# Adaptive max pooling on one core: both large stores moved to ScalarE's DMA queue, in another order and another cut

## The chip, the cores and the metric

The kernel runs on one core of one Trainium2 chip. The core has engines with queues of their own; three of them matter here. VectorE (DVE in the profile) does all the arithmetic. SyncE (SP) and ScalarE (ACT) only issue transfers; the profile calls their DMA queues q1 and q10. Both queues are served by the same 16 DMA engines. TensorE does nothing, and GpSimd only writes a few constants at the start.

The metric is the device time of one execution in microseconds. The kernel before takes 334.97 us (median of 3 runs, 334.92 to 335.0).

## The reference

```python
batch, channels, length = 32, 256, 4096      # float32
output_size = 256

for i in range(output_size):
    start = int(i * length / output_size)
    end = int((i + 1) * length / output_size)
    result[:, :, i] = np.max(x[:, :, start:end], axis=-1)
```

4096 / 256 = 16, so every window has exactly W = 16 elements and no two overlap. The input is 134.22 MB, the output 8.39 MB. One output number is the maximum of 16 neighbouring float32 numbers, 64 bytes.

## The kernel before

**Tiling.** All 2,097,152 windows are numbered in order of memory and dealt out over the 128 partitions, `total` = 16384 windows to a partition. They come in two groups, each contiguous in memory. In group A a partition holds 13436 windows: loads of 128 (`FIRST`), twelve of 1024 (`CHUNK`) and one of 1020. In group B it holds 2948: two loads of 1024 and one of 900 (`last`). A load brings the same number of windows to every partition, one row to each; a row of 1024 windows is 65,536 bytes, the 900 windows are 57,600 bytes. Within group A the loads run from the end of each row to its front, within group B from front to end.

**Buffers.** `ring` holds two slots of 1176 windows (1024 + `GAP` = 152). Loads other than the first alternate between the two slots, and within a slot between its lower and its upper end (`moved`), so that a load overlaps only a part of what the load two before it left there. `kept` holds the maxima of everything but the last load, 15484 numbers per partition. The maxima of the last load go into the top of its own slot in `ring` (`last_kept`), beside what is being read.

**Reductions.** `pooled` (line 54) is one VectorE instruction, `reduce_max` over the 16 elements of each of n windows. A full load is reduced by two of them, of 872 and 152 windows, the one first whose region the next load into that slot needs. The last load is reduced by one of 900.

**Order of issue.** SyncE issues the first load (line 87), then the 16 others (line 96), each when the reduction that frees its region is done and the earlier load of that region has landed. Behind the last load on the same queue it issues the two stores of `kept` (line 117): first group A's (13436 numbers or 53,744 bytes a row, 6.88 MB), whose maxima have long been there, and then group B's first 2048 numbers (8,192 bytes a row, 1.05 MB), when the load before the last has been reduced. ScalarE issues one transfer in the whole kernel (line 114): the store of the last 900 numbers (3,600 bytes a row, 0.46 MB), when the last reduction is done. `tc.no_sync_barrier()` between them is a line for the scheduler of the program, not an instruction; the semaphores that order engines and transfers are put in by the framework from the regions that each operation reads and writes.

**Names for the end of the kernel.** Counted without `FIRST`, loads have numbers 0 to 15 (`n_loads`); number 14 is "the load before the last", number 15, with the 900 windows, "the last load". The long store is group A's.

Of the kernel before, what the change touches and what calls it, by code (L numbers as in the profile page):

```python
# [1 line left out]

# [4 lines left out]


@with_exitstack
def kernel(  # L10
    ctx: ExitStack,
    tc: tile.TileContext,
    x: bass.AP,
    output_size: bass.AP,
    out: bass.AP,
):

    nc = tc.nc
    P = nc.NUM_PARTITIONS
    fp32 = mybir.dt.float32

    B, C, L = x.shape
    O = int(output_size)  # L30
    assert L % O == 0, (L, O)
    W = L // O
    total = B * C * O // P
    assert B * C * O % P == 0

    CHUNK = 1024
    GAP = 152
    FIRST = 128
    LOADS_A, LOADS_B = 13, 2

    LESS = 4
    group_a = [FIRST] + [CHUNK] * (LOADS_A - 1) + [CHUNK - LESS]
    last = total - sum(group_a) - LOADS_B * CHUNK
    group_b = [CHUNK] * LOADS_B + [last]
    assert 0 < last and last * (W + 1) <= CHUNK * W

    pool = ctx.enter_context(tc.tile_pool(name="pool", bufs=1))
    ring = pool.tile([P, 2 * (CHUNK + GAP) * W], fp32, tag="ring", name="ring")
    kept = pool.tile([P, total - last], fp32, tag="kept", name="kept")

    xw = x.flatten_outer_dims().rearrange("r (o w) -> (r o) w", w=W)
    ow = out.flatten_outer_dims().rearrange("r o -> (r o)")

    def pooled(dst, at, n):

        nc.vector.reduce_max(  # L56
            out=dst,
            in_=ring[:, at * W : (at + n) * W].rearrange("p (n w) -> p n w", w=W),
            axis=mybir.AxisListType.X,
        )  # L60

    taken = 0

    def group(n):

        nonlocal taken
        span = slice(taken * P, (taken + n) * P)
        taken += n
        return (
            xw[span].rearrange("(p n) w -> p (n w)", p=P),  # L70
            ow[span].rearrange("(p n) -> p n", p=P),
        )

    stores = []
    n_loads = 0
    base = 0
    for g, loads in enumerate((group_a, group_b)):
        xg, og = group(sum(loads))
        a = sum(loads) if g == 0 else 0
        for n in loads:  # L80
            if g == 0:
                a -= n
            xn = xg[:, a * W : (a + n) * W]
            dst = kept[:, base + a : base + a + n] if n != last else None
            if n == FIRST:

                nc.sync.dma_start(  # L87
                    out=ring[:, CHUNK * W : (CHUNK + n) * W], in_=xn
                )
                pooled(dst, CHUNK, n)  # L90
            else:

                low = n_loads % 2 * (CHUNK + GAP)
                moved = n_loads // 2 % 2
                at = low + moved * GAP
                nc.sync.dma_start(out=ring[:, at * W : (at + n) * W], in_=xn)
                if n != last:
                    cut = CHUNK - GAP if moved else GAP
                    parts = [(0, cut), (cut, n)]
                    for u, v in parts if moved else parts[::-1]:  # L100
                        pooled(dst[:, u:v], at + u, v - u)
                else:
                    end = (at + CHUNK) * W
                    last_kept = ring[:, end - n : end]
                    pooled(last_kept, at, n)
                n_loads += 1
            if g:
                a += n
        full = a - last if g else sum(loads)
        stores.append((og[:, 0:full], kept[:, base : base + full]))  # L110
        base += full
    assert taken == total

    nc.scalar.dma_start(out=og[:, full : full + last], in_=last_kept)
    tc.no_sync_barrier()
    for dst, src in stores:
        nc.sync.dma_start(out=dst, in_=src)


# [1 line left out]
_INS = ['x', 'output_size']  # L121
_OUTS = [((32, 256, 256), 'float32')]

_NUMBERS = {'output_size': 256}


# [26 lines left out]
```

## Time and profile before

| | us |
|---|---|
| median of the times | 334.97 |
| span of the profiled execution, first to last instruction | 333.1 |
| what the median has beyond that span | 1.9 |
| VectorE busy (83% of the span) | 276.5 |
| VectorE idle, waiting for loads | 51.5 |
| the last load: issued, landed | 290.99, 21.6 later |
| the long store: issued, landed | 291.37, 37.2 later |
| the 1.05 MB store: issued, landed | 312.94, 18.1 later |
| the 0.46 MB store: issued, landed | 328.00, 4.2 later |

Times within the profile count from its first instruction. The profile has its own single execution; its time is the span with what lies around it, so sums are made against 333.1 and the 1.9 us are added. Busy time is an instruction's own time; the DMA's share is the mean over 16 engines. A transfer's time to landing runs from its issue on the queue to the last of its completion records, waiting in the queue included. A row of a transfer is one packet on one DMA engine, and each transfer leaves one 4-byte record per engine as well: 128 + 16 = 144 packets.

### The profile page before, as it was taken

To read this page: it belongs to the slowest core of one execution; us is meant where nothing else is said; L and a number is where in the kernel's file an instruction comes from. 1 tells how busy PE (TensorE), PEld (TensorE's weight loads), DVE (VectorE), ACT (ScalarE), POOL (GpSimd) and SP (SyncE) were. 2 spreads that over 40 slices of the span, in tenths; PEclk is the share of its full clock that TensorE was granted. 3 is DMA by queue.
4 is the path that set the end of the run, shared out by engine and by line. 5 is a ranking of instruction groups with operands and counts; after the bars stand their busy time and mean duration, and the time that the engine had idled before them with its cause. 6 is when DMAs were issued, how large, how long until landed. Compare 5 with 4: busy or idle time off the path is not lost.

```text
span 333.1 us, 113 instructions
## 1 busy us (share of the span) xinstructions
DVE 276.5 (83%) x32; POOL 0.2 (0%) x4
## 2 busy tenths in 40 slices
DVE  2009979797997979799797979979797998979993
POOL 0000000000000000000000000000000000000000
DMA  9898989899898989899898989899898989899996
GB/s 378 378 504 378 504 378 496 386 441 441 378 504 378 504 378 496 386 457 425 378 504 378 504 378 504 378 441 441 385 494 377 504 378 504 378 458 443 421 413 285
DMA packets 2880, 142.61 MB, mean 428 GB/s; under 512 B 320, under 2 KB 320, under 8 KB 448
## 3 DMA queue, kind: packets, MB, share of 16 engines
q1 hardware_dynamic: 2736, 142.15, 98.8%
q10 hardware_dynamic: 144, 0.46, 0.3%
HBM read 134.22 MB, written 8.39 MB: 428 GB/s over the span
## 4 chain that ended last, share of the span: by engine, by line
DMA 57%; DVE 36%; DVEq 5%; issue 0%; SPq 0%
DMA ring<-in_x_dram 57%; DVE kept L56 36%; DVEq L148 5%; SPq L87 0%
## 5 line engine op out<-in xcount | busy, mean ns | idle before, releaser
L56 DVE TENSOR_REDUCE kept<-ring 128x152 f32<-128x2432 f32 (+3 forms) x31 | 261.4, 8472 | 51.5 <-DMA ring<-in_x_dram 51.5
L56 DVE TENSOR_REDUCE ring<-ring 128x900 f32<-128x14400 f32 x1 | 15.1, 15144 | 0.0
L134 POOL MEMSET const-bfloat16-1.0<- 128x1 bf16 x1 | 0.1, 102 | 0.0
L134 POOL MEMSET const-uint8-127<- 128x1 uint8 x1 | 0.1, 102 | 0.0
L134 POOL MEMSET const-float32-0.0<- 128x1 f32 x1 | 0.1, 99 | 0.2 <-issue 0.2
L134 POOL MEMSET const-float32-1.0<- 128x1 f32 x1 | 0.1, 99 | 0.0
## 6 DMA issues: line engine op xcount, KB each, us to landing
ring<-in_x_dram SPq DMA_DIRECT2D x1, 8160.0 KB, 23.9
ring<-in_x_dram SPq DMA_DIRECT2D x1, 7200.0 KB, 21.6
out_dram<-kept SPq DMA_DIRECT2D x1, 6718.0 KB, 37.2
ring<-in_x_dram SPq DMA_DIRECT2D x1, 1024.0 KB, 4.7
out_dram<-kept SPq DMA_DIRECT2D x1, 1024.0 KB, 18.1
out_dram<-ring ACTq DMA_DIRECT2D x1, 450.0 KB, 4.2
ring<-in_x_dram SPq DMA_DIRECT2D x14, 24.0
```

The costliest lines, as they stand in the source:

```text
L56: nc.vector.reduce_max(out=dst, in_=ring[:, at * W : (at + n) * W].rearrange("p (n w) -> p n w", w=W), axis=mybir.AxisListType.X,)
L134: nc = _bacc.Bacc("TRN2", target_bir_lowering=False, num_devices=1)
L148: with _tile.TileContext(nc) as tc:
```

## The change

Three things change at the end of the kernel.

1. The load before the last is cut at 828 (`OPEN`) and 196 (`late`) windows instead of 872 and 152. The maxima of the 828 go into `kept` as before; those of the 196 go into the top of the last load's slot in `ring`, just ahead of the 900 maxima of the last load. So `last_kept` is now 1096 numbers long. The order of the windows on VectorE is the same.
2. Group B's first store is now 1024 + 828 = 1852 numbers a row (7,408 bytes, 0.948 MB) and needs only the reduction of the 828. The last store is 1096 numbers a row (4,384 bytes, 0.561 MB). The long store keeps its rows.
3. Queues and order: ScalarE issues group B's first store and then, behind it, the long store. SyncE, behind the last load, issues only the last store.

```diff
+    OPEN = 828
+    late = CHUNK - OPEN
     kept = pool.tile([P, total - last], fp32, tag="kept", name="kept")
+    assert last * (W + 1) + late <= CHUNK * W
...
                 nc.sync.dma_start(out=ring[:, at * W : (at + n) * W], in_=xn)
-                if n != last:
+                if n_loads == LOADS_A + LOADS_B - 1:
+                    pooled(dst[:, 0:OPEN], at, OPEN)
+                    opened = at + OPEN
+                elif n != last:
                     cut = CHUNK - GAP if moved else GAP
                     parts = [(0, cut), (cut, n)]
                     for u, v in parts if moved else parts[::-1]:
                         pooled(dst[:, u:v], at + u, v - u)
                 else:
                     end = (at + CHUNK) * W
-                    last_kept = ring[:, end - n : end]
-                    pooled(last_kept, at, n)
+                    last_kept = ring[:, end - n - late : end]
+                    pooled(last_kept[:, 0:late], opened, late)
+                    pooled(last_kept[:, late:], at, n)
                 n_loads += 1
             if g:
                 a += n
-        full = a - last if g else sum(loads)
+        full = a - last - late if g else sum(loads)
         stores.append((og[:, 0:full], kept[:, base : base + full]))
...
-    nc.scalar.dma_start(out=og[:, full : full + last], in_=last_kept)
+    nc.scalar.dma_start(out=stores[1][0], in_=stores[1][1])
     tc.no_sync_barrier()
-    for dst, src in stores:
-        nc.sync.dma_start(out=dst, in_=src)
+    nc.scalar.dma_start(out=stores[0][0], in_=stores[0][1])
+    nc.sync.dma_start(out=og[:, full : full + late + last], in_=last_kept)
```

## The prediction

> **What bounds the kernel now.** I read the page first, then the DMA queues in short windows of the tail, then the vector engine's instructions by shape, and last the first microseconds, for how long an issued transfer takes to reach the DMA engines.
>
> ```profile
> DVE 276.5 (83%) x32; POOL 0.2 (0%) x4
> ...
> DMA  9898989899898989899898989899898989899996
> q1 hardware_dynamic: 2736, 142.15, 98.8%
> q10 hardware_dynamic: 144, 0.46, 0.3%
> ...
> out_dram<-kept SPq DMA_DIRECT2D x1, 6718.0 KB, 37.2
> ...
> out_dram<-kept SPq DMA_DIRECT2D x1, 1024.0 KB, 18.1
> out_dram<-ring ACTq DMA_DIRECT2D x1, 450.0 KB, 4.2
> ```
>
> These are lines of the page. The 16 DMA engines are busy 98.8% + 0.3% = 99.1% of a 333.1 us span; the missing 0.9% is 3.0 us. VectorE is busy 83% and is the bound nowhere but, perhaps, at the very end. q1 is SyncE's queue, q10 ScalarE's: 2736 is 19 transfers of 144 packets, so each engine gets 8 rows and one 4-byte record of completion per transfer.
>
> The page's chain of waits names DMA and VectorE alternately and hides that the DMA never rests; the windows show it. Columns: stretch and length, VectorE and GpSimd busy, TensorE's clock, DMA share, GB/s. A packet is counted where it starts, so only stretches with small rows, or whole rounds of long ones, read as shares.
>
> ```profile
> 0.00:1.72 1.72, 0.00 (x0) 0.20 (x4) 1.00 0.00 0
> 1.72:2.30 0.58, 0.00 (x0) 0.00 (x0) 1.00 1.14 240
> ...
> 309.50:310.05 0.55, 0.55 (x1) 0.00 (x0) 1.00 4.17 1676
> 310.10:311.84 1.74, 1.74 (x2) 0.00 (x0) 1.00 0.00 0
> 311.84:312.30 0.46, 0.46 (x1) 0.00 (x0) 1.00 4.34 1869
> 327.70:328.15 0.45, 0.27 (x1) 0.00 (x0) 1.00 0.88 364
> 328.15:330.20 2.05, 0.00 (x0) 0.00 (x0) 1.00 1.00 420
> 330.20:330.56 0.36, 0.00 (x0) 0.00 (x0) 1.00 0.85 338
> 330.57:331.72 1.15, 0.00 (x0) 0.00 (x0) 1.00 0.79 313
> 331.72:333.10 1.38, 0.00 (x0) 0.00 (x0) 1.00 0.00 0
> ```
>
> The 3.0 us are 1.7 before the first packet and 1.4 after the last one (331.72). Between them there is nothing to win by order alone. In the tail: the 16 engines take up the last row of the last load at 309.50 to 310.05, and none starts anything until 311.84; from 311.84 to 312.30 each goes straight on to the long store (6.88 MB), which has been queued since its issue at 291.37. By queue, 311.84 to 327.7 holds 144 packets at 434 GB/s: 15.85 us for the long store. At 327.70 to 328.15 the engines go on to the 1.05 MB store, at 330.20 to 330.56 to the last one, on q10. So 2.45 us and, to 331.72, 1.15 us. The last lands at its issue, 328.00, plus 4.2 = 332.2; 0.9 us of closing follow.
>
> ```profile
> L56 DVE TENSOR_REDUCE kept<-ring 128x872 f32<-128x13952 f32 x14 | 205.6, 14686 | 44.0 <-DMA ring<-in_x_dram 44.0
> L56 DVE TENSOR_REDUCE kept<-ring 128x152 f32<-128x2432 f32 x15 | 40.1, 2676 | 0.0
> L56 DVE TENSOR_REDUCE ring<-ring 128x900 f32<-128x14400 f32 x1 | 15.1, 15144 | 0.0
> ```
>
> ```profile
> 295.63 17.28 DVE L56 TENSOR_REDUCE kept<-ring 128x872 f32<-128x13952 f32 x2 [2.07 <-DMA ring<-in_x_dram]
> 312.82 15.14 DVE L56 TENSOR_REDUCE ring<-ring 128x900 f32<-128x14400 f32 x1
> ```
>
> VectorE, by shape and in order of time: 872 + 152 windows of the load before the last, then the 900 of the last, with no idle time ahead of them; done at 327.96.
>
> **The change part by part.** The profiled span of 333.1 lies 1.87 us under the median of 334.97; I add the same 1.87 to the forecast span.
>
> *The reductions.* A window costs (14686 - 2676)/720 = 16.68 ns, so 828 windows take 14686 - 44 x 16.68 = 13952 ns and 196 take 3410 ns. Three instructions and 1924 windows as before: the 900 still start at 312.82 if the last load has landed by then (it does so at 290.99 + 21.6 = 312.6) and end at 327.96. The 196 now write into the ring; a wait of VectorE on itself for that may cost between 0 and some 0.1 us (the 900 have such a write already and start without idle time). I take 0.
>
> *The first store on ScalarE.* The 828 end at 295.63 + 13.95 = 309.58; ScalarE issues 0.04 later, as it does now behind the 900 (327.96 to 328.00): 309.62, for 0.37 us. How long until its rows are at the engines? Nearest row: the first load, issued at 0.73, shows its first packets from 1.72 to 2.30, 1.0 to 1.6 us later. Farthest: the last store, issued at 328.00, shows its first at 330.20, 2.2 us. The first gives 310.6 to 311.2, the second 311.8. In either case the engines have the last row in hand, since they took it up by 310.05 and let go of it from 311.84 on. I take the first row, as there nothing stands in the way; hole in the DMA: 0, and by the second reading at most some 0.3 us on the last engines.
>
> *The long store, now second on ScalarE.* It loses its place behind the last load on q1, held since 291.37, and is issued at about 310.0 to 310.4, at the engines by 312.2 at the latest. The first store's 0.948 MB (1852 windows) cover them for 2.45 x 1852/2048 = 2.22 us, until 314.06 to 314.52. So it costs nothing; without that cover it would be up to 0.4 us. Then 15.85 us: 329.91 to 330.37. ScalarE has nothing else to do, so its wait holds up nothing but these two; SyncE no longer stands behind the 152 windows to issue a store.
>
> *The last store, now on SyncE.* 1096 windows, 0.561 MB: 1.15 x 1096/900 = 1.40 us, against 1.15 + 2.45 - 2.22 = 1.38 that byte and packet counts leave (same bytes, same number of rows as before). Issued at 328.00, at the engines 329.0 to 329.6, or 330.2 by the far row; needed at 329.91 to 330.37. Cost 0, at the far end some 0.2 us. Its packets end at about 331.3 to 331.75, it lands at 332.2, the span ends at 333.1.
>
> The far row has two readings: from 328.15 to 330.20 all 105 packets were q1's, so either the store came late or it was there and q1's transfer was finished first. The Trainium skill ("DMA: Bandwidth & Descriptors", Queues, rings and completion order) says that a DMA engine takes turns between queues only after a whole packet of some 9 to 17 descriptors, and a share here has 9. By that rule the store had been there and waited, and the sum is +0; by the other reading it is +0.2 to +0.3 us. No run here tells the two apart.
>
> Sum: 0, between -0.15 (below) and +0.5 us: **335.0 us**, its own range 334.7 to 335.5.
>
> **The rivals.**
>
> *Slower: the last load's records wait behind the new store.* Now two queues hold work when the engines finish the last load. The 4-byte record that reports the load is q1's, and the first store's rows are there before it is sent. If an engine serves q10's 8 rows first, the load lands 2.22 us later, at 314.8; the 900 end at 329.99, the last store is issued at 330.03, at the engines 331.0 to 331.6, which have been dry since 329.91 to 330.37. End of packets 331.6 + 1.4 = 333.0, span 334.4, **336.2 us**; 337 with 2.2 us to the engines. It decides only once the load lands later than about 313.6 (330.37 - 1.57 - 0.04 - 15.14); a turn of one row (2.22/8 = 0.28 us) does nothing. Against it: those 105 packets of q1, 0 of q10, at a time when q10's store should have been there. For it: that store may not have been there.
>
> *Slower: the hand-over runs dry,* that is, the rows are not ready while the last row is in hand. The queue ahead of the engines was 20 us deep and is now 0.6 to 1.2 us (311.84 less 310.6 to 311.2). From an issue-to-engine time of 2.7 us on, all engines idle, and each further microsecond is one at the end, as the last store's own delay hides behind it. At 3.5 us: 0.8 us, **335.8 us**. Against it: 2.2 us is the most that the trace shows, and that may be a wait in turn.
>
> *Faster.* The rows of the last load took 2.13 us each in the round before (60.9% of 3.5 us) but 2.29 in the last round (4.17 x 0.55): the change from reading to writing costs 0.16 us now, with 53.7 KB rows queued behind. Short rows behind it may spare that: -0.15, **334.8 us**, which is still no change that can be told. For more than 0.2% (0.67 us) the 19.9 us of the tail would have to run 3.4% faster, while share and rate show neither a hole nor a row that is slow for its size.
>
> **How the numbers follow.** 0.2%, 0.67 us, is about what a measurement of this kernel tells from no change. Forecast, with the small gain counted in (within 0.2%): 0.78. Records behind the store, 336.2: 0.09. Hand-over dry, 335.8: 0.07. A tail faster by over 0.2%, below 334.3, by something that I do not see: 0.06. So 0.06 faster, 0.78 same, 0.16 slower. The range runs from the gain's end with a little more, 334.5, to the first slower case, 336.2.
>
> **What would show it.** Right: no stretch without DMA work between 309 and 331.7; q10's first packets of 7.4 KB follow the last load's rows at 311.8 to 312.3; the last load lands at about 312.6 and the 900 start at 312.8 to 313.0; the long store's rows start by 314.5; q1's last 4.4 KB rows follow from 329.9 to 330.4; span 333.1. Wrong: the last load landing later than 313.6, idle time of VectorE ahead of the 900, a DMA share below 1 at 312 or at 330, or long rows that take other than 15.85 us in all.

## The result, and the profile after

The changed kernel takes 335.65 us (median of 11 runs, 335.54 to 335.86) where the kernel before takes 334.98 (11 runs): a ratio of 1.0021, with a 95% interval of 1.0013 to 1.0029. It is slower by 0.67 us, which is just the 0.2% that was taken for the limit of what can be told. The 335.0 forecast were 0.65 too low; the time lies within the range.

From the page of the changed kernel:

```profile
span 333.8 us, 112 instructions
...
DMA  9898989898998989898989989898989899899996
...
q1 hardware_dynamic: 2592, 134.78, 93.5%
q10 hardware_dynamic: 288, 7.83, 5.5%
...
out_dram<-kept ACTq DMA_DIRECT2D x1, 6718.0 KB, 21.6
...
out_dram<-kept ACTq DMA_DIRECT2D x1, 926.0 KB, 6.1
out_dram<-ring SPq DMA_DIRECT2D x1, 548.0 KB, 5.0
```

The shares of the queues add up to 99.0% of 333.8 us, 330.5 us; before, 99.1% of 333.1 was 330.1. So the DMA engines as a body are hardly busier. The order of time at the end (start, length, engine, line, what):

```profile
295.48 13.95 DVE L64 TENSOR_REDUCE kept<-ring 128x828 f32<-128x13248 f32 x1 [2.06 <-DMA ring<-in_x_dram]
309.35 18.47 DVE L64 TENSOR_REDUCE ring<-ring 128x196 f32<-128x3136 f32 x2
309.46 0.37 ACTq L126 DMA_DIRECT2D out_dram<-kept  x1
309.87 3.11 ACTq L128 DMA_DIRECT2D out_dram<-kept  x1
327.85 0.35 SPq L129 DMA_DIRECT2D out_dram<-ring  x1
```

VectorE's side came out as forecast: 13.95 us for the 828 windows, no idle time ahead of the 196 or the 900, and the last store issued at 327.85, 37.0 us after the last load (290.85), as before (328.00 and 290.99). The last store then lands 5.0 us after its issue where it took 4.2, at 332.85 instead of 332.2: all of the loss is between that issue and that landing. What stands out is the 3.11 us that ScalarE spends on issuing the long store.

The same execution in windows (stretch and length, VectorE, GpSimd, clock, DMA share, GB/s):

```profile
309.50:310.05 0.55, 0.55 (x1) 0.00 (x0) 1.00 3.88 1676
311.60:312.05 0.45, 0.45 (x1) 0.00 (x0) 1.00 1.09 264
312.05:314.00 1.95, 1.95 (x2) 0.00 (x0) 1.00 0.93 391
314.00:314.40 0.40, 0.40 (x1) 0.00 (x0) 1.00 4.98 2145
314.40:315.05 0.65, 0.65 (x1) 0.00 (x0) 1.00 0.05 23
315.05:315.15 0.10, 0.10 (x1) 0.00 (x0) 1.00 1.25 537
...
331.85:332.35 0.50, 0.00 (x0) 0.00 (x0) 1.00 0.04 18
```

And by queue, from 311.60 to 312.05 and from 312.05 to 313.90 (packets, MB, share of 16 engines):

```profile
q10 hardware_dynamic: 16, 0.12, 107.0%
q1 hardware_dynamic: 16, 0.00, 2.0%
```

```profile
q10 hardware_dynamic: 98, 0.73, 93.0%
```

In 311.60 to 312.05 every engine finishes the last load, sends its record (q1's 16 small packets) and takes up the first row of ScalarE's store. These 16 rows take 107.0% x 0.45 = 0.48 us each; the rows behind them 93.0% x 1.85 x 16 / 98 = 0.28. So a first row takes 0.20 us longer, on the mean; a packet's time runs from when its engine takes it up, so the engine counts as busy while it waits. That is why no hole shows. One of the 16 can be singled out, from 311.965 to 311.970 (a packet's whole time is put where it starts, hence the share over 100%):

```profile
q10 hardware_dynamic: 1, 0.01, 1488.8%
```

That is 1488.8% x 0.005 x 16 = 1.19 us for one row, 0.9 too long; with seven more rows its engine would be done with the first store at 315.1. One engine is indeed that far behind the rest: by 314.40 fifteen have gone on to the long store, and the sixteenth does so only after 315.05 (the window 314.40 to 315.05 holds its last two short rows and nothing else). Its eight rows at 0.28 us take 2.25, so its data began to move at about 312.85, 3.4 us after the issue at 309.46. With 15.85 us for the long store and eight rows of the last store at 0.17 us it would be done at 315.10 + 15.85 + 1.4 = 332.3, and at the far end one engine is again alone, in 331.85 to 332.35. So this one engine sets the end.

### The profile page after: what moved, and what is told of

It reads as the page before. It is cut to its first block, busy times and chain, and to the rows that moved or that the text cites. A ratio compares the mean times of both kernels' runs of the same rounds, so it can differ in the third digit from the quotient of the medians.

```text
span 333.8 us, 112 instructions
## 1 busy us (share of the span) xinstructions
DVE 276.5 (83%) x32; POOL 0.2 (0%) x4
## 4 chain that ended last, share of the span: by engine, by line
DMA 57%; DVE 36%; DVEq 5%; issue 0%; SPq 0%
DMA ring<-in_x_dram 57%; DVE kept L64 35%; DVEq L160 5%; DVE ring L64 1%; SPq L95 0%
## 5 line engine op out<-in xcount | busy, mean ns | idle before, releaser
L64 DVE TENSOR_REDUCE kept<-ring 128x152 f32<-128x2432 f32 (+4 forms) x30 | 258.1, 8641 | 51.4 <-DMA ring<-in_x_dram 51.4
L64 DVE TENSOR_REDUCE ring<-ring 128x196 f32<-128x3136 f32 (+1 forms) x2 | 18.5, 9276 | 0.0
## 6 DMA issues: line engine op xcount, KB each, us to landing
ring<-in_x_dram SPq DMA_DIRECT2D x1, 8160.0 KB, 23.9
ring<-in_x_dram SPq DMA_DIRECT2D x1, 7200.0 KB, 21.6
out_dram<-kept ACTq DMA_DIRECT2D x1, 6718.0 KB, 21.6
```

The source lines that it names most:

```text
L64: nc.vector.reduce_max(out=dst, in_=ring[:, at * W : (at + n) * W].rearrange("p (n w) -> p n w", w=W), axis=mybir.AxisListType.X,)
```

## The experiments

All times are compared with runs of the kernel before on the same chip (medians of 334.95 to 335.08 us). The numbers in brackets are the 95% interval of the ratio; 0.0009 of it is 0.3 us, so differences of 0.1 or 0.2 us between two runs mean nothing by themselves. Each edit is against the changed kernel.

### SyncE issues all three stores

```diff
-    nc.scalar.dma_start(out=stores[1][0], in_=stores[1][1])
+    nc.sync.dma_start(out=stores[1][0], in_=stores[1][1])
...
-    nc.scalar.dma_start(out=stores[0][0], in_=stores[0][1])
+    nc.sync.dma_start(out=stores[0][0], in_=stores[0][1])
```

> Cut and order of the changed kernel, but SyncE issues all three stores: first store, long store, last store. Changed kernel 335.65 us, before 334.98. Theory 'jam' (the long store's issue, which took 3.11 us on ScalarE, blocks the descriptors of the store ahead of it for one DMA engine, whatever the queue): SyncE's second issue also takes about 3 us and one engine's first row is 0.9 us late, 335.6. Theory 'queue change' (an engine that goes over from q1 to another queue pays, one of them 0.9 us): everything stays on q1, nobody pays, 335.0. Theory 'too late' (the rows come only 2.2 us ahead of their use): same as changed, 335.6.

335.06 us, 0.11 over before (ratio 0.9995 to 1.0012). From its order of time:

```profile
309.63 0.35 SPq L126 DMA_DIRECT2D out_dram<-kept  x1
310.03 0.43 SPq L128 DMA_DIRECT2D out_dram<-kept  x1
```

Cut, order and lead are the changed kernel's, and the loss is gone: it lies with the queue. The long store is issued in 0.43 us. The first rows of 7.4 KB take 0.29 us: 311.70 to 311.98 holds 11 of them and 11 records at a share of 72.4%, 3.24 us of packets. Both "too late" and "jam" expected a loss here whatever the queue, and are wrong in that form.

### The long store back on SyncE

```diff
-    nc.scalar.dma_start(out=stores[0][0], in_=stores[0][1])
+    nc.sync.dma_start(out=stores[0][0], in_=stores[0][1])
```

> Cut of the changed kernel; ScalarE issues the first store alone, SyncE the long store (right behind the last load, at about 291) and then the last store. 'Jam': ScalarE has no second issue, so no row is late: 335.0. 'Queue change': the engines go over to q10 and back somewhere, one of them pays 0.7 to 0.9 us: 335.6. 'Too late': the long store fills the time until the rows are there, 335.0.

335.05 us, 0.10 over before (0.9995 to 1.0013): nobody pays, though ScalarE's queue is used. The windows 311.7 to 313.7 and 313.70 to 316.00 by queue bear on something that the prediction rested on:

```profile
q1 hardware_dynamic: 32, 0.86, 99.9%
```

```profile
q1 hardware_dynamic: 16, 0.86, 86.3%
q10 hardware_dynamic: 16, 0.12, 12.2%
```

In the first window each engine takes up one long row behind the load's record, and none of ScalarE's, issued at 309.53. In the second they take 16 long rows and 16 short ones, and on to 329.7 it is 112 and 116. With work on two queues the engines here take turns row by row. They do not finish one queue's share of a transfer first, and a store issued some 2.2 us ahead is not yet in the turn.

### Earlier: OPEN = 700

```diff
-    OPEN = 828
+    OPEN = 700
```

> The changed kernel with OPEN = 700 instead of 828: the first store (5.6 KB rows) is issued 128 x 16.68 ns = 2.1 us earlier, at about 307.3, with one more row of the last load to come. 'Too late': no row is late any more, 335.0. 'Jam': the long store's issue on ScalarE takes about 5 us instead of 3.1, and one engine still starts late, 335.6. 'Queue change': same as changed, 335.6. If the engines change queues in the middle of a transfer's rows, the first store's rows start ahead of the last load's last row and the load lands up to 1.7 us late; nothing comes of it as long as the last reduction starts before 313.6.

335.22 us, 0.27 over before (0.9999 to 1.0017). Issued at 307.60, the first rows take their normal time, 64.0% x 0.26 x 16 / 10 = 0.27 us for rows of 6.9 KB. ScalarE's second issue took 4.47 us, nearly the 5 that "jam" expected, yet the first rows are not late. That speaks for "too late" and against the jam. The last load lands 21.9 us after its issue instead of 21.6: its record has to let one short row of q10 pass, as turns by row demand.

### The cut alone

```diff
-    nc.scalar.dma_start(out=stores[1][0], in_=stores[1][1])
+    nc.scalar.dma_start(out=og[:, full : full + late + last], in_=last_kept)
     tc.no_sync_barrier()
-    nc.scalar.dma_start(out=stores[0][0], in_=stores[0][1])
-    nc.sync.dma_start(out=og[:, full : full + late + last], in_=last_kept)
+    for dst, src in stores:
+        nc.sync.dma_start(out=dst, in_=src)
```

> The cut alone (828 and 196 windows, 7.4 KB and 4.4 KB rows); queues and order as before: SyncE the long store and then the first store, ScalarE the last one. All theories: 335.0, as before. If it gives 335.6, the cut is the cause and not the queues.

334.94 us against 334.95 (0.9992 to 1.0009). The cut and its shorter rows are worth nothing, either way.

### ScalarE's queue used once before

```diff
-                nc.sync.dma_start(
+                nc.scalar.dma_start(
                     out=ring[:, CHUNK * W : (CHUNK + n) * W], in_=xn
                 )
```

> The changed kernel (335.65 us, one engine's first 7.4 KB row 0.9 us late), but the very first load of the kernel comes from ScalarE, so that its queue q10 has been used once, long before. Theory 'first use' (an engine is late because q10 is used for the first time): no late row, 335.0. Theories 'jam' (the long store's issue is stuck 3.1 us behind the first store on ScalarE) and 'too late' (q10's rows need over 2.2 us to be in place on the slowest engine): no change, 335.6. The first load's 8 KB rows may alternate with those of the second load and land at 20 us or so instead of 5; the first reduction comes later by that, which the 2 us of idle time per load take up.

338.34 us (1.0082 to 1.0113), worse by another cause. The first load landed 24.8 us after its issue instead of 4.6, as its rows took turns with the long ones of the second load; the first reduction began at 25.6, and the DMA share fell to 0.65 from 40 to 44 us. I had thought that the idle time of VectorE takes this up, and it does not. So its time says nothing on the question. Its trace does. By queue, 313.50 to 314.50, which holds 14 of the 16 first rows of the first store in this run:

```profile
q10 hardware_dynamic: 14, 0.10, 68.6%
```

68.6% x 1.0 x 16 / 14 = 0.78 us for a first row, though q10 had been used at the kernel's start: it is not the first use. The other way round it falls too: with OPEN = 764 or 700, and with short rows in hand, q10 is used for the first time and is not late. In this run the late rows do not lengthen the tail: the first store lands 24.0 us after the last load's issue (312.44 + 5.4 - 293.82), as in the kernels without a loss, and not 24.7 as in the changed kernel. By this, late rows cost time only where they make the slowest engine later.

### The last store on ScalarE too

```diff
-    nc.sync.dma_start(out=og[:, full : full + late + last], in_=last_kept)
+    nc.scalar.dma_start(out=og[:, full : full + late + last], in_=last_kept)
```

> The changed kernel with the last store on ScalarE too, behind the long one: no change of queue at the end. The changed kernel's last store had first rows of 0.26 to 0.32 us where 0.17 is the rule, and SyncE's kernel (all on q1) none. 'Change of queue costs 0.1 us at the end, the late engine 0.7': 335.5. If the late engine has its cause at the end and not at the first store: 335.0.

335.84 us, 0.76 over before (1.0013 to 1.0030). Without the change of queue at the end the loss is still there; the first rows of the first store (311.8 to 312.45) take 109.8% x 0.65 = 0.71 us, on the mean. The cause lies at the first store.

### The first store alone on ScalarE

```diff
-    nc.scalar.dma_start(out=stores[0][0], in_=stores[0][1])
-    nc.sync.dma_start(out=og[:, full : full + late + last], in_=last_kept)
+    nc.sync.dma_start(out=og[:, full : full + late], in_=last_kept[:, 0:late])
+    tc.no_sync_barrier()
+    nc.sync.dma_start(out=stores[0][0], in_=stores[0][1])
+    nc.sync.dma_start(
+        out=og[:, full + late : full + late + last], in_=last_kept[:, late:]
+    )
```

> ScalarE issues the first store alone; nothing stands behind it on either queue until SyncE, when the 196 windows are reduced (312.8), issues three stores: those 196 (784 B rows), the long one, the last 900. 'Jam': without a second issue on ScalarE no first row of 7.4 KB is late (none over 0.5 us). 'Too late': the same engine is late again, with a first row of about 1.2 us. The time is not the test: the long store is issued at 313.2 and the first store ends at 314.1, so 0.1 to 1.3 us without DMA work are added in any case, 335.1 to 336.3, and 0.9 more on one engine only if the late row is there and not hidden by that.

335.92 us, 0.84 over before (1.0016 to 1.0033). By queue, 311.80 to 312.38:

```profile
q10 hardware_dynamic: 16, 0.12, 117.8%
```

117.8% x 0.58 = 0.68 us for a first row, with no second issue behind it. So the jam on ScalarE is not the cause; that it is another effect of the same thing is likely and not shown.

### Earlier by half as much: OPEN = 764

```diff
-    OPEN = 828
+    OPEN = 764
```

> The changed kernel with OPEN = 764: the first store is issued 64 x 16.68 ns = 1.07 us earlier than with 828, 3.2 to 3.6 us ahead of its first use instead of 2.2 to 2.5. With 828 the time was 335.65, with 700 335.22. 'Too late': with 3.2 us no first row is late, 335.0 to 335.2. 'Jam': the late row of 0.9 us is there as with 828, 335.6.

335.36 us, 0.28 over before (0.9999 to 1.0017). The issue at 308.74, some 3.2 us ahead of its first use, is early enough, and an issue earlier by another microsecond (OPEN = 700) gains nothing more. Whether the 0.28 that are left are a cost at all is open: the interval reaches down to no change.

### OPEN = 764, and the last store on ScalarE

```diff
-    OPEN = 828
+    OPEN = 764
...
-    nc.sync.dma_start(out=og[:, full : full + late + last], in_=last_kept)
+    nc.scalar.dma_start(out=og[:, full : full + late + last], in_=last_kept)
```

> OPEN = 764 (first store 1.07 us earlier, 335.36 alone, 0.28 over its kernel before) and the last store on ScalarE too, behind the long store. Theory 'a queue that stood idle behind long rows starts late' (lead of 2.2 to 2.5 us is too short for such a queue, 3.2 us is enough; a queue that is at work needs no more than 2.1): neither the first store's first rows nor the last store's are long, and the time is 0.0 to 0.15 us over before, 335.0 to 335.2. If the 0.28 come from the earlier issue itself (the last load's record waits behind a row of the first store, landing 0.5 us later), they stay: 335.3.

335.01 us, 0.04 over before (0.9993 to 1.0010): with both taken away no cost is left that can be told. By queue, 311.70 to 311.98 of this kernel:

```profile
q10 hardware_dynamic: 13, 0.09, 80.1%
```

80.1% x 0.28 x 16 / 13 = 0.28 us, a row's normal time. The last store's first rows differ too. On SyncE's idle queue with OPEN = 764 (329.99 to 330.27, 10 rows of q1 at 70.5%) they took 0.32 us; here, on the queue that has just sent the long store (329.82 to 330.05, 12 rows and 11 records at 61.4%), 0.18. That the last load's record comes later costs nothing: it landed 22.0 us after its issue here too. But neither do the longer first rows of the last store show as the cause of the 0.28: in the profiled execution with OPEN = 764 the last store lands 41.2 us after the last load's issue (328.32 + 4.1 - 291.19), here 41.3 (328.21 + 4.1 - 291.05), in the kernel before 41.2 (328.00 + 4.2 - 290.99). What is longer there lies ahead of the last load, which is issued at 291.19 instead of 290.99, and there the two kernels are the same.

### Short rows in hand

```diff
-                nc.sync.dma_start(out=ring[:, at * W : (at + n) * W], in_=xn)
+                for u, v in ((0, 700), (700, n)) if n == last else ((0, n),):
+                    nc.sync.dma_start(
+                        out=ring[:, (at + u) * W : (at + v) * W],
+                        in_=xn[:, u * W : v * W],
+                    )
```

> The changed kernel (OPEN = 828, +0.67 us), but the last load is issued in two pieces of 700 and 200 windows, so that the engines have rows of 12.8 KB (0.48 us each) in hand and not of 57.6 KB (2.13 us) when the first store is issued. 'Idle queue behind long rows': with short rows in hand the first store's rows are in place in time, no first row over 0.35 us, +0.2 (the last store's 0.1 stays). 'Idle queue alone', whatever stands in front: first rows of up to 1.2 us again, +0.7.

335.32 us, 0.35 over before (0.9999 to 1.0017). From its order of time, and by queue from 311.80 to 312.08:

```profile
309.60 0.37 ACTq L130 DMA_DIRECT2D out_dram<-kept  x1
310.01 0.44 ACTq L132 DMA_DIRECT2D out_dram<-kept  x1
```

```profile
q10 hardware_dynamic: 12, 0.09, 75.9%
```

Issued as late as in the changed kernel, the first rows take 75.9% x 0.28 x 16 / 12 = 0.28 us, and the second issue is not stuck. So in these runs the idle queue is late only when the engines have long rows in hand. That fits the kernel before, whose last store on the idle q10 follows rows of 8 KB: its first 27 rows of 3.6 KB took 66.5% x 0.36 x 16 / 27 = 0.14 us each in 330.20 to 330.56, no longer than the later ones.

### Later: OPEN = 872

```diff
-    OPEN = 828
+    OPEN = 872
```

> The changed kernel with OPEN = 872, the cut of the kernel before: the first store is issued 44 x 16.68 ns = 0.73 us later. 'Too late': the time until its rows move stays what it is, so every engine stands idle for about 0.73 us more, and the time goes from +0.67 to +1.2 to +1.4 us, 336.2 to 336.4. 'A fixed price of the change of queue': no change, +0.7.

335.76 us, 0.79 over before (1.0015 to 1.0034). From 311.70 to 312.50:

```profile
q10 hardware_dynamic: 16, 0.12, 144.1%
```

Now a first row takes 144.1% x 0.8 = 1.15 us on the mean, 0.87 too long on every engine. That every engine pays more is what "too late" expected; that the time is only 0.12 longer than with 828, no difference that can be told, is not. The slowest engine is no later than before: measured from the last load's issue, the first store lands 24.7 us later (310.54 + 5.3 - 291.17), as with 828 (309.46 + 6.1 - 290.85). So the lead that an engine needs is not one fixed time: some 2.3 us here on the mean (issue 310.54, taken up at about 312.0, 0.87 waited), 3.4 for the slowest with 828. What sets it on one engine is open.

### SyncE and ScalarE swapped in every transfer

```diff
-                nc.sync.dma_start(
+                nc.scalar.dma_start(
                     out=ring[:, CHUNK * W : (CHUNK + n) * W], in_=xn
                 )
...
-                nc.sync.dma_start(out=ring[:, at * W : (at + n) * W], in_=xn)
+                nc.scalar.dma_start(out=ring[:, at * W : (at + n) * W], in_=xn)
...
-    nc.scalar.dma_start(out=stores[1][0], in_=stores[1][1])
+    nc.sync.dma_start(out=stores[1][0], in_=stores[1][1])
     tc.no_sync_barrier()
-    nc.scalar.dma_start(out=stores[0][0], in_=stores[0][1])
-    nc.sync.dma_start(out=og[:, full : full + late + last], in_=last_kept)
+    nc.sync.dma_start(out=stores[0][0], in_=stores[0][1])
+    nc.scalar.dma_start(out=og[:, full : full + late + last], in_=last_kept)
```

> The changed kernel with SyncE and ScalarE swapped in every transfer: ScalarE issues all loads and the last store, SyncE the first store and the long one. If it is the idle queue that starts late, SyncE's first rows are now as long as ScalarE's were (up to 1.2 us), +0.7. If it is ScalarE or its queue, no first row is over 0.35 us: +0.1 to +0.3.

335.71 us, 0.74 over before (1.0014 to 1.0032). In 311.80 to 312.33 SyncE's first rows now take 130.3% x 0.53 = 0.69 us, and it is SyncE that is stuck in the second issue:

```profile
309.80 0.37 SPq L126 DMA_DIRECT2D out_dram<-kept  x1
310.22 2.99 SPq L128 DMA_DIRECT2D out_dram<-kept  x1
```

```profile
q1 hardware_dynamic: 16, 0.12, 130.3%
```

It is the idle queue and not the engine that issues.

The kernels side by side. Issue and landing are counted from the issue of the last load, each landing being the sum of issue and time to landing, from the one profiled execution; the last column is the time over the kernel before. The engines finish the last load's rows some 21.0 us after its issue (311.60 to 312.05 less 290.85 in the changed kernel), so a first store issued at 18.6 has a lead of some 2.4 us. In the kernel before the last store lands at 41.2.

| kernel | queue of the first store | rows in hand | first store issued | first store lands | last store lands | over before |
|---|---|---|---|---|---|---|
| all on SyncE | at work | 57.6 KB | 18.6 | 23.9 | 41.2 | +0.11 |
| OPEN = 700 | idle | 57.6 KB | 16.5 | 23.8 | 41.3 | +0.27 |
| OPEN = 764, all on ScalarE | idle | 57.6 KB | 17.6 | 24.0 | 41.3 | +0.04 |
| OPEN = 764 | idle | 57.6 KB | 17.6 | 23.9 | 41.2 | +0.28 |
| short rows in hand | idle | 12.8 KB | 18.6 | 24.0 | 41.3 | +0.35 |
| changed kernel | idle | 57.6 KB | 18.6 | 24.7 | 42.0 | +0.67 |
| all on ScalarE | idle | 57.6 KB | 18.6 | 24.4 | 41.7 | +0.76 |
| first store alone on ScalarE | idle | 57.6 KB | 18.6 | 24.4 | 41.8 | +0.84 |
| swapped | idle | 57.6 KB | 18.6 | 24.6 | 41.9 | +0.74 |
| OPEN = 872 | idle | 57.6 KB | 19.4 | 24.7 | 41.8 | +0.79 |

In the upper five the first store lands at 23.8 to 24.0 us and the last one at 41.2 to 41.3, as in the kernel before; in the lower five the first lands at 24.4 to 24.7 and the last at 41.7 to 42.0. Within a group the times differ by about as much as they are uncertain, and part of that lies ahead of the last load: it is issued at 290.85 in the changed kernel and at 291.31 with all stores on ScalarE, which differ only behind it. None of the runs beats the kernel before: its engines are never idle, and order alone wins nothing, as the sum had it.

## Why the prediction was right, and where not

**The bound, and "no change" as the likeliest: right in substance.** The order of the stores is free, as the DMA's work is the same: the version with both delays taken away is at +0.04 us, the cut alone at -0.01. The sum of 0 holds for the parts that it has. That the measured 335.65 still lies within the full range is in part luck: its upper end, 336.2, was taken from another rival, the records behind the store, which did not happen; the sum's own range ended at 335.5.

**The reductions: right.** 13.95 us, the 900 without idle time ahead of them, the last store issued 37.0 us after the last load.

**The first store on ScalarE: this step failed.** I took 1.0 to 1.6 us from issue to engine, from the first load of the kernel, "as there nothing stands in the way", and thereby chose the wrong of two rows: in the tail a 57.6 KB row stands in the way on every engine. The far row, 2.2 us, was nearer to the truth and still too short: 2.3 to 2.6 us on the mean and 3.4 on the slowest engine. I bounded the hole by "some 0.3 us on the last engines"; it was 0.20 on the mean, but 0.9 on one, and the slowest of 16 sets the end. That is why the forecast's own range ended short of the 335.65.

**The long store behind it: harmless, but not as said.** I had it at the engines by 312.2 at the latest; its issue alone took 3.11 us, to 312.98. The first store's rows cover that, as the sum had it: fifteen engines went on to the long store at 314.0 to 314.4.

**The weighed rule: wrongly applied.** By the Trainium skill ("DMA: Bandwidth & Descriptors", Queues, rings and completion order) a whole packet of typically some 9 to 17 descriptors is drained before an engine turns to another queue. I took an engine's share of a transfer, 8 rows and a record, for one such packet and weighed the reading that the last store had been at the engines early and had waited. The run with the long store on SyncE shows turns by single rows, 16 to 16 in 2.3 us and 112 to 116 in 16 us. How many descriptors a row has is in no trace here, so the figure itself is not tested; that a share is drained at a stretch is refuted. With turns by rows, the 105 packets of q1 with none of q10 suggest the other reading: the store was not yet in the turn until 2.2 us after its issue. No run tests that with rows of 8 KB. Read that way, the rival of the hand-over would have been likelier than the 0.07 that I gave it.

**The rivals.** "The hand-over runs dry" named the place and the cause, a lead of about 2 us where it had been 20. It expected that all engines stand idle from 2.7 us on, at 0.8 us for 3.5; it was mainly one engine, at 3.4 us, and the time grew by 0.67. "The records wait behind the new store" did not happen: the load landed at 290.85 + 21.6. Where the store came earlier, with OPEN = 700 or 764, the record did wait, by one row, 0.3 us, which I had put down as harmless. "Faster" had the rows right and the gain wrong: the last rows of the load took 3.88 x 0.55 = 2.13 us instead of 2.29. But 0.16 us less on the mean is no gain at the end even where the first short rows are not late: with all stores on SyncE the last rows took 2.37 x 0.90 = 2.13 us too (309.40 to 310.30), and the time is +0.11. Why the rows were longer before is open: with the long store back on SyncE, 53.7 KB rows stand behind them again, and they took 2.40 x 0.90 = 2.16.

**The last store on SyncE: nearly right.** Behind long rows, on a queue idle since the last load, its first rows take 0.1 us and more too long (0.32 us instead of 0.18 with OPEN = 764). That this lengthens the kernel is not shown: the last store lands at 41.2 us in that kernel as before.

## What to carry to other kernels

A transfer that is to take over without a gap from rows of some 50 KB must be issued early if its queue stands idle: here 2.4 us were too few, 3.4 enough; on the queue that is already at work 2.4 were enough. A time from issue to first packet, taken where the DMA is idle, is no price for one where it is loaded; look for a row under load, and judge by the slowest of the 16 engines, as a mean share hides one that is late. In a DMA-bound kernel moving stores between queues can lose this lead and, with no idle time to fill, gains nothing.

## What the runs showed of the hardware

- A row that waits counts as busy: an engine's first row on the idle queue took 0.48 to 1.15 us on the mean instead of 0.28, and 1.19 on one engine of the changed kernel, and left no hole in the DMA share. The lateness shows only in the mean time of the first packets and in the spread of the engines.
- Two queues take turns row by row, in both pairs that were seen: 7.4 KB beside 53.7 KB (112 rows to 116 in 16 us), and an 8 KB load beside 64 KB rows, which landed after 24.8 us instead of 4.6.
- The second transfer on an idle queue, with 57.6 KB rows in hand, holds its issuing engine: 3.11 us on ScalarE, 2.99 on SyncE, 4.47 when issued earlier; 0.43 on a queue at work, 0.44 with 12.8 KB rows in hand. In this kernel that engine had nothing else to do.
- Why the data of the first store begin to move some 2.6 us after the issue on the mean and 3.4 us on one engine of the changed kernel, and what an engine does with a new queue's rows while a long row runs, is not settled by these runs.
